# Stored key order inside each block of 128, one transfer back from DRAM instead of four, and an issue order that counts transfers instead of pieces

## The chip, the cores and the metric

The kernel runs on one core of one Trainium2 chip. The metric is the device time of one execution in microseconds (us); for the kernel before the change three runs gave 772.27, 773.07 and 774.95, median 773.07. Five engines work side by side, each with its own queue of instructions: PE (TensorE, matrix products), DVE (VectorE), ACT (ScalarE), POOL (GpSimd) and SP (SyncE). In this kernel SP does nothing but issue DMA transfers, all of them.

## The reference

One layer of a streaming encoder, for a prompt of 1024 positions and a sample of 32, in float32. `A` heads use band attention with a relative bias and a softmax, `B` heads use stick-breaking attention. Keys and values are also outputs.

```python
def band_attention(q, k, v, q_pos, k_pos, bias_table):
    s = jnp.einsum('bqhd,bkhd->bhqk', q, k).astype(jnp.float32) * ATTN_SCALE
    ...
    w = jax.nn.softmax(s, axis=-1).astype(v.dtype)
    return jnp.einsum('bhqk,bkhd->bqhd', w, v)

def stick_breaking(q, k, v, q_pos, k_pos):
    z = jnp.einsum('bqhd,bkhd->bhqk', q, k).astype(jnp.float32) * ATTN_SCALE
    causal = (k_pos[None, :] < q_pos[:, None])[None, None]
    log_beta = jax.nn.log_sigmoid(z)
    log_1m = jnp.where(causal, jax.nn.log_sigmoid(-z), 0.0)
    after = lax.cumsum(log_1m, axis=3, reverse=True) - log_1m
    w = jnp.where(causal, jnp.exp(log_beta + after), 0.0).astype(v.dtype)
    return jnp.einsum('bhqk,bkhd->bqhd', w, v)

def finish(h, oa, ga, ob, gb, w_out, g_post, p, w_ple, w_ple_gate):
    y = jnp.concatenate([oa * jax.nn.silu(ga), ob * jax.nn.silu(gb)], axis=-1) @ w_out
    h = h + rmsnorm(y, g_post)
    return h + jax.nn.sigmoid(h @ w_ple_gate) * (p @ w_ple)
```

In front of these stands an RMS norm and one projection to q, k, v and a gate for 8 `A` heads and 8 `B` heads of 64 columns.

## The kernel before

[...] Stage 0 norms and transposes x and starts the projection; stages 1 to 8 (`rec.stage`) each hold two attention heads of one kind (A, B, A, B ...) woven with the projection columns of the next pair, and in stage 8 with the gates; stages 9 to 13 are the output projection and the final gate. Names in the profile say the kind: `mm_kB` is a projection bank, `SB` a bank of scores, `ptwB` a bank of transposed weights, `PVB` the bank of weights times values.

**Weights and their transposition.** In a head the 1024 queries are eight blocks `i` of 128. `scores(i)` makes the scores of block `i` against up to 1024 keys (up to 640 for `A`) and from them the weights `w1` with queries on the partitions: for `A` a DVE reduction and an ACT exponential, for `B` two ACT sigmoids per bank, a DVE scan, and a POOL multiplication `be<-be`. Products with the values need the keys on the partitions, so `weights_t(i)` transposes, in one of two ways set by `ROUND`. Blocks `A` 0 to 4 and `B` 0 to 3 and 7 are transposed by PE into `ptw` banks. Blocks `A` 5, 6, 7 and `B` 4, 5, 6 (48 in all) go through DRAM: DVE turns squares of 32 by 32, one DMA stores the block (`swapA<-be`), and four DMAs bring it back (`be<-swapA`), one for each group of 32 keys, each to 32 partitions. ACT (`wTh<-be`) and DVE (`wTl<-be`) then split it. The values of each of the eight pairs make the same trip in `values_out` (`swapA<-vxA`, then four `stvA<-swapA`) and are then stored to the output by one DMA, `out_dram<-vt`.

**Order.** The program isn't run in the order in which it is written. A recorder collects all instructions with their dependences; `latest` works out a due time for each, and `simulate` then places them one at a time, per engine, by due time plus an offset from two tables (`AHEAD_OF`, and by stage `AHEAD_AT`), with estimated costs. `PASSES` is how often due times and placement are made anew. For SP, the planner before holds back a transfer while the pieces of those under way are over a limit:

```python
while away and (away[0][0] <= t or flying + o.pieces > AWAY):
    landed, pieces = heapq.heappop(away)
    flying -= pieces
    t = max(t, landed)
```

The queues are then fixed: an instruction that isn't ready holds up all that stand behind it on its engine. In the program as built each transfer also takes one of eight completion semaphores in turn, and SP waits before it issues a transfer until the one that had the semaphore before it is complete.

Of the kernel before, what the change touches and what calls it, by code (L numbers as in the profile page):

```python
# [10 lines left out]
AF = mybir.ActivationFunctionType  # L11
ALU = mybir.AluOpType

P = 128
# [14 lines left out]
    ('ACT', 'L'): -809, ('ACT', 'Qfs'): -495, ('ACT', 'S'): -671, ('ACT', 'be'): 45,  # L29
    ('ACT', 'gT'): 1145, ('ACT', 'junk'): -1222, ('ACT', 'o'): 225, ('ACT', 'oT'): -1406,  # L30
    ('ACT', 'om'): -82, ('ACT', 'ot'): -967, ('ACT', 'p'): -874, ('ACT', 'pleo'): -1053,
    ('ACT', 'sgg'): 65, ('ACT', 'stq'): -314, ('ACT', 'stv'): -824, ('ACT', 'v'): 55,
    ('ACT', 'wTh'): -117, ('ACT', 'whS'): 246, ('ACT', 'whs'): 933, ('ACT', 'x'): -696,
    ('ACT', 'xS'): -616, ('DVE', 'Kl'): -588, ('DVE', 'L'): 544, ('DVE', 'S'): -85,
    ('DVE', 'Vl'): -913, ('DVE', 'cc'): -493, ('DVE', 'diags'): -1253, ('DVE', 'g'): 212,
    ('DVE', 'h'): -1097, ('DVE', 'hnl'): 570, ('DVE', 'lg'): 343, ('DVE', 'om'): -53,
    ('DVE', 'ot'): -267, ('DVE', 'over'): 483, ('DVE', 'sgg'): -356, ('DVE', 'sq'): 277,
    ('DVE', 'stats'): -1190, ('DVE', 'uu'): 246, ('DVE', 'v'): -653, ('DVE', 'vx'): -722,
    ('DVE', 'w'): -1469, ('DVE', 'wTl'): 37, ('DVE', 'wl'): 652, ('DVE', 'wlS'): -1002,
# [3 lines left out]
    ('POOL', 'be'): 196, ('POOL', 'gT'): 309, ('POOL', 'o'): -123, ('POOL', 'ogg'): 890,  # L43
    ('POOL', 'om'): 197, ('POOL', 'rs'): -497, ('POOL', 's'): -1046, ('POOL', 'sgg'): 929,
# [4 lines left out]
}  # L49
AHEAD_AT = {  # L50
    (0, 'ACT', 'pleo'): 1195, (0, 'ACT', 'sq'): 1380, (0, 'ACT', 'stk'): -1095, (0, 'ACT', 'v'): 1160,
    (0, 'DVE', 'hnl'): -45, (0, 'DVE', 'rb'): 799, (0, 'DVE', 'sq'): 461, (0, 'DVE', 'x'): 572,
# [12 lines left out]
    (4, 'ACT', 'om'): -35, (4, 'ACT', 'wTh'): -365, (4, 'ACT', 'whs'): -1064, (4, 'DVE', 'S'): -89,  # L65
    (4, 'DVE', 'Ss'): 1254, (4, 'DVE', 'ot'): 307, (4, 'DVE', 'wTl'): -134, (4, 'PE', 'S'): 77,
    (4, 'PE', 'ptw'): 56, (4, 'PE', 'ptws'): -349, (4, 'POOL', 'ksS'): -959, (4, 'POOL', 'om'): 162,
    (4, 'POOL', 'w'): -151, (4, 'POOL', 'wl'): 1076, (4, 'SP', 'Kcs'): 477, (4, 'SP', 'be'): -112,
    (4, 'SP', 'o'): -577, (4, 'SP', 'wr'): -890, (5, 'ACT', 'be'): -546, (5, 'ACT', 'kd'): -484,
    (5, 'ACT', 'stk'): 1450, (5, 'ACT', 'wTh'): -482, (5, 'DVE', 'S'): -110, (5, 'DVE', 'om'): -127,  # L70
# [3 lines left out]
    (6, 'ACT', 'L'): 734, (6, 'ACT', 'be'): -459, (6, 'ACT', 'kd'): 409, (6, 'ACT', 'stv'): 1412,  # L74
# [4 lines left out]
    (7, 'ACT', 'om'): 64, (7, 'ACT', 'stk'): -573, (7, 'ACT', 'wTh'): -208, (7, 'DVE', 'Kcs'): 660,  # L79
# [6 lines left out]
    (8, 'POOL', 'ogg'): -1077, (8, 'POOL', 'om'): 190, (8, 'POOL', 'sgg'): -350, (8, 'POOL', 'w'): 324,  # L86
# [2185 lines left out]
```

## Time and profile before

| what | value |
|---|---|
| median of three runs | 773.07 us |
| the profiled execution: its time, its span | 773.43 us, 771.7 us |
| PE busy (matmuls) | 758.4 us, 98% |
| DVE, ACT, POOL busy | 611.6, 525.0, 447.2 us |
| DMA queue q1 | 172.70 MB, 77.1% of 16 engines' span |
| granted TensorE clock | 1.00 |

The page gives for each engine the time that it was busy. A matmul's end is modelled, so "busy" PE isn't yet PE at its pace: how fast matmuls follow one another is seen from their starts. SP isn't listed as busy on the page; its issues are seen in the timeline, as SPq. "Waits" rows say which engine and tile waited, for whom, for how long in all, how often, and how long at most. An issue row gives the size and the median time from issue to landing.

### The profile page before, as it was taken

How to read it: one execution, taken by the hardware profiler on the slowest of the kernel's cores; microseconds unless marked ns; L12 is line 12 of the kernel's file. 1: busy time of each engine (PE TensorE's matmuls, PEld its weight loads, DVE VectorE, ACT ScalarE, POOL GpSimd, SP SyncE). 2: the span in 40 equal slices, each digit the busy share in tenths (PEclk: the TensorE clock that was granted, in tenths of full speed). 3: DMA queues.
4: the chain of work that ended last, by engine and by line, in shares of the span. 5: the costliest groups of instructions: out<-in, count | busy, mean ns of one | idle time of the engine just before them, and what ended most of it. 6: DMA issues, size and time to landing. Idle time of an engine off the chain costs nothing.

```text
span 771.7 us, 14284 instructions
## 1 busy us (share of the span) xinstructions
PE 758.4 (98%) x4410; PEld 698.9 (91%) x4410; DVE 611.6 (79%) x1067; ACT 525.0 (68%) x1122; POOL 447.2 (58%) x503
## 2 busy tenths in 40 slices
PE   9999999999999999999999999999999999999997
PEld 7999999999989899999999999999998877888786
DVE  7837868878878898959898698698565688988965
ACT  6656776787766776866788586665347877884641
POOL 6624434751356682557874467679463448689533
PEclk9999999999999999999999999999999999999999
DMA  8658667476789858889799989897779866769664
GB/s 302 220 146 223 178 166 218 120 197 206 182 192 253 218 171 229 258 237 263 216 240 269 246 231 223 270 276 214 213 267 300 275 221 227 235 202 332 214 212 136
DMA packets 202333, 173.61 MB, mean 225 GB/s; under 512 B 66817, under 2 KB 164457, under 8 KB 202258
## 3 DMA queue, kind: packets, MB, share of 16 engines
q1 hardware_dynamic: 202258, 172.70, 77.1%
q8 instruction: 35, 0.57, 0.3%
q14 instruction: 40, 0.33, 0.1%
HBM read 105.46 MB, written 58.78 MB: 213 GB/s over the span
## 4 chain that ended last, share of the span: by engine, by line
PE 86%; DVE 4%; DMA 4%; SPq 3%; issue 1%; ACT 1%; DVEq 0%; POOL 0%; ACTq 0%; POOLq 0%
PE mm_gA L780 6%; PE mm_gB L780 6%; PE mm_kA L780 6%; PE mm_qA L780 5%; PE mm_kB L780 5%; PE mm_vA L780 5%; PE mm_qB L780 4%; PE PVB L780 4%; PE mm_vB L780 4%; PE SB L780 4%; PE PVA L780 3%; PE ple L780 3%; PE SA L780 3%; SPq L780 3%; PE g0P L780 3%; PE g2P L780 3%
## 5 line engine op out<-in xcount | busy, mean ns | idle before, releaser
L780 POOL TENSOR_TENSOR be<-be 128x128 f32<-128x128 f32 (+8 forms) x66 | 85.1, 1294 | 48.6 <-DVE be L780 23.0
L780 DVE TENSOR_TENSOR_SCAN be<-be,SB 128x384 f32<-128x384 f32 (+5 forms) x96 | 91.5, 963 | 8.2 <-ACT be L780 4.3
L780 ACT ACTIVATE be<-SB 128x384 f32<-128x384 f32 (+4 forms) x192 | 83.4, 497 | 18.2 <-DVE be L780 7.0
L780 DVE TENSOR_TENSOR wTl<-be,wTh 128x640 fp32r<-128x640 f32 (+2 forms) x48 | 51.9, 1086 | 11.2 <-ACT wTh L780 7.8
L780 ACT ACTIVATE be<-be,statA 128x640 f32<-128x640 f32 (+3 forms) x64 | 44.5, 696 | 11.6 <-DVE statA L780 11.5
L780 DVE STREAM_TRANSPOSE be<-be 128x640 f32<-128x640 f32 (+3 forms) x56 | 47.9, 866 | 3.4 <-POOL be L780 2.3
L780 ACT CAST wTh<-be 128x640 fp32r<-128x640 f32 (+2 forms) x48 | 37.6, 784 | 13.2 <-DMA be<-swapB 7.3
L780 PE MATMUL SB<-kdB,LB 128*128 128x384 f32 (+5 forms) x96 | 33.7, 354 | 0.4 <-issue 0.3
L780 PE MATMUL SB<-klB,LB 128*128 128x384 f32 (+5 forms) x96 | 33.3, 347 | 0.0
L780 DVE CUSTOM_DVE_ANT_0 be<-SA,biasA 128x320 f32<-128x320 f32 (+3 forms) x64 | 29.7, 481 | 4.4 <-PE SA L780 3.4
L780 POOL TENSOR_TENSOR gB<-gB,gB 128x256 f32<-128x256 f32 x32 | 26.9, 861 | 9.8 <-DMA gB<-in_w_ple_gate_dram 7.9
L780 ACT CAST wTh<-ptwB 128x512 fp32r<-128x512 f32 (+3 forms) x48 | 22.4, 484 | 13.0 <-PE PVB L780 8.0
L780 PE MATMUL SA<-kdA,LA 128*128 128x320 f32 (+2 forms) x96 | 30.3, 325 | 0.2 <-PE mm_kB L780 0.2
L780 PE MATMUL SA<-klA,LA 128*128 128x320 f32 (+2 forms) x96 | 30.1, 317 | 0.0
L780 POOL TENSOR_TENSOR oB<-oB,oB 128x256 f32<-128x256 f32 x32 | 25.6, 826 | 6.7 <-DMA oB<-in_w_out_dram 4.8
L780 PE MATMUL ptwB<-ident,be 128*128 128x128 f32 x144 | 26.5, 274 | 2.4 <-ACT be L780 1.0
L780 POOL TENSOR_TENSOR klB<-stkB,kdB 64x1024 fp32r<-64x1024 f32 x8 | 20.0, 2504 | 14.0 <-ACT kdB L780 12.1
L780 DVE TENSOR_TENSOR wTl<-ptwB,wTh 128x512 fp32r<-128x512 f32 (+3 forms) x48 | 25.0, 540 | 3.9 <-ACT wTh L780 3.7
L780 POOL TENSOR_TENSOR klA<-stkA,kdA 64x1024 fp32r<-64x1024 f32 (+2 forms) x9 | 19.3, 2150 | 14.4 <-ACT kdA L780 9.5
L780 DVE TENSOR_TENSOR wTl<-ptwA,wTh 128x128 fp32r<-128x128 f32 (+3 forms) x48 | 21.8, 478 | 5.3 <-ACT wTh L780 3.5
L780 DVE TENSOR_TENSOR LA<-stqA,LA 64x1024 fp32r<-64x1024 f32 (+2 forms) x9 | 15.6, 1730 | 11.9 <-ACT LA L780 11.8
L780 POOL TENSOR_TENSOR wl_vB<-wr_vB,wh_vB 128x512 fp32r<-128x512 f32 x8 | 10.5, 1309 | 24.5 <-DMA stvA<-swapA 13.3
(694 smaller groups left out, 2653.6 us busy)
## 6 DMA issues: line engine op xcount, KB each, us to landing
swapA<-be SPq DMA_DIRECT2D x24, 320.0 KB, 3.7
be<-swapA SPq DMA_DIRECT2D x96, 80.0 KB, 3.0
oB<-in_w_out_dram SPq DMA_DIRECT2D x16, 256.0 KB, 4.2
sum_dro<-oB SPq DMA_DIRECT2D x16, 256.0 KB, 3.2
gB<-in_w_ple_gate_dram SPq DMA_DIRECT2D x16, 256.0 KB, 3.9
sum_drg<-gB SPq DMA_DIRECT2D x16, 256.0 KB, 3.8
x<-in_x_prompt_dram SPq DMA_DIRECT2D x16, 256.0 KB, 3.9
h_dr<-h SPq DMA_DIRECT2D x8, 512.0 KB, 4.3
```

The costliest lines, as they stand in the source:

```text
L780: getattr(getattr(tc.nc, o.what[0]), o.what[1])(*args, **kw)
```

## The change

Three things change together.

1. **Key order.** Inside each block of 128 keys, key `32 c + q` now stands at place `4 q + c`. With it the four DMAs of a block become one to 128 partitions, for the 48 blocks of weights and for the eight pairs of values: 56 x 4 = 224 loads become 56. The store of values to the output, which must be in the old order, becomes four DMAs from every fourth partition in place of one: 8 become 32. In all, 970 DMAs become 826; the bytes and the pieces stay.
2. **Where PE transposes,** the weights must stand in the new order in `w1` before. For `A` 0 to 4 the exponential writes every fourth element (`mixed`), for `B` 0 to 3 and 7 the second sigmoid does, and the POOL multiplication reads one operand and writes its result so. These are 40 exponentials, 48 sigmoids and 40 multiplications.
3. **The planner** counts eight transfers (`LANES`) in place of pieces, has other DMA and issue constants, makes four passes in place of one, and both offset tables are new. So the order changes on every engine and in every stage. The instructions of PE, DVE, ACT and POOL are the same in number.

```diff
 AHEAD_OF = {
-    ('ACT', 'L'): -809, ('ACT', 'Qfs'): -495, ('ACT', 'S'): -671, ('ACT', 'be'): 45,
+    ('ACT', ''): 326, ('ACT', 'S'): -178, ('ACT', 'be'): 37, ('ACT', 'g'): 1215,
...
-ISSUE = 550
+ISSUE = 480
 TABLE = 1280
-DMA_START, DMA_DONE, DMA_RATE, DMA_MARGIN = 1950, 300, 320.0, 2000
-AWAY = 1900
+DMA_START, DMA_DONE, DMA_RATE, DMA_MARGIN = 1850, 1600, 320.0, 2100
+LANES = 8
...
-PASSES = 1
+PASSES = 4
...
-                while away and (away[0][0] <= t or flying + o.pieces > AWAY):
-                    landed, pieces = heapq.heappop(away)
-                    flying -= pieces
-                    t = max(t, landed)
+                if len(landed) >= LANES:
+                    t = max(t, landed[-LANES])
                 free[e] = t + o.busy
                 line = max(line, t + DMA_START) + o.late
-                heapq.heappush(away, (line + DMA_DONE, o.pieces))
-                flying += o.pieces
+                landed.append(line + DMA_DONE)
...
-            for c in range(4):
-                part = D[:, c * 256:(c + 1) * 256].rearrange("(g t) x -> t g x", t=32)
-                dma(st[32 * c:32 * c + 32, 0:SEQ].rearrange("t (g x) -> t g x", g=4), part)
+            dma(st[:, 0:SEQ].rearrange("p (g x) -> p g x", g=4), D.rearrange("(g t) (c x) -> (t c) g x", t=32, c=4))
...
-            later(o_p[0, 0, :, h2, :].rearrange("(b p) h d -> p b (h d)", p=P), out[:, b0:8, :])
+            rows = o_p[0, 0, :, h2, :].rearrange("(b c q) h d -> c q b (h d)", c=4, q=32)
+            for c in range(4):
+                later(rows[c], out[c::4, b0:8, :])
...
+    def split(x):
+        return x.rearrange("p (b c q) -> p b c q", c=4, q=32)
+
+    def mixed(x):
+        return x.rearrange("p (b q c) -> p b c q", c=4, q=32)
...
+                mix = mixed if i not in together else lambda x: x
                 for a, b, s in pieces:
-                    nc.scalar.activation(w1[:, a:b], s, AF.Sigmoid)
+                    nc.scalar.activation(mix(w1[:, a:b]), split(s) if i not in together else s, AF.Sigmoid)
...
-                nc.gpsimd.tensor_tensor(w1[:, 0:n], w1[:, 0:n], w0[:, 1:n + 1], ALU.mult)
+                if i in together:
+                    nc.gpsimd.tensor_tensor(w1[:, 0:n], w1[:, 0:n], w0[:, 1:n + 1], ALU.mult)
+                else:
+                    nc.gpsimd.tensor_tensor(mixed(w1[:, 0:n]), mixed(w1[:, 0:n]), split(w0[:, 1:n + 1]), ALU.mult)
...
-                nc.scalar.activation(w1[:, 0:n], w0[:, 0:n], AF.Exp, bias=m[:, last:last + 1], scale=-1.0, accum_out=r)
+                out, src = w1[:, 0:n], w0[:, 0:n]
+                if i not in together:
+                    out, src = mixed(out), split(src)
+                nc.scalar.activation(out, src, AF.Exp, bias=m[:, last:last + 1], scale=-1.0, accum_out=r)
...
-                for c in range(4):
-                    x = dr[:, c * m * 32:(c + 1) * m * 32].rearrange("(g k) x -> k g x", k=32)
-                    dma(w1[32 * c:32 * c + 32].rearrange("k (g x) -> k g x", g=4), x)
+                dma(w1.rearrange("p (g x) -> p g x", g=4), dr.rearrange("(g k) (c x) -> (k c) g x", k=32, c=4))
```

Two places show how rows move. The first is SP's queue in stage 5, at the second `A` head of pair 2, where the blocks 5, 6 and 7 of its weights come back (`swapA21_5` to `_7`; `x4` at a row's end is four DMAs). Before:

```order
L780 DMA swapA21_7_145<-be_178 128x640
L780 DMA o_dr2_65<-otA21_0_0_4359 64x256
L780 DMA klB21_4299<-klB21_4299 64x1024
L780 DMA be_178<-swapA21_5_143 32x4x160 x2
L780 DMA sum_dro_81<-oB212_4342 128x512
L780 DMA o_dr2_65<-otA20_1_0_4250 64x256
L780 DMA be_178<-swapA21_5_143 32x4x160 x2
L780 DMA oB123_4455<-in_w_out_dram 128x512
L780 DMA be_178<-swapA21_6_144 32x4x160 x4
L780 DMA oB223_4461<-in_w_out_dram 128x512
L780 DMA be_178<-swapA21_7_145 32x4x160 x4
```

The same place after:

```order
L767 DMA swapA21_7_145<-be_178 128x640
L767 DMA sum_dro_81<-oB212_4174 128x512
L767 DMA klB21_4284<-klB21_4284 64x1024
L767 DMA oB123_4335<-in_w_out_dram 128x512
L767 DMA oB223_4336<-in_w_out_dram 128x512
L767 DMA biassA1_4305<-r_dr_83 32x544
L767 DMA wr_vA3_0_4371<-in_w_in_dram 128x4x128
L767 DMA biassA1_4305<-r_dr_83 32x544
L767 DMA be_178<-swapA21_5_143 128x4x160
L767 DMA be_178<-swapA21_6_144 128x4x160
L767 DMA be_178<-swapA21_7_145 128x4x160
```

From the first load of block 5 to the last of block 7 there were 16 issues; now there are three, and most of the transfers that stood between them stand ahead of them.

The second place is ACT's queue a little later, where the first `B` head of pair 2 starts (`SB20_0` to `SB20_4` are its banks of scores) and the returned `A` weights are split (`wTh<-be`). Before:

```order
L780 ACTIVATE be_178<-SB20_0_0_4493 128x128
L780 ACTIVATE be_178<-SB20_1_0_4494 128x256
L780 CAST wTh_693<-be_178 128x4x5x32
L780 ACTIVATE be_178<-SB20_0_0_4493 128x128
L780 ACTIVATE be_178<-SB20_1_0_4494 128x256
L780 ACTIVATE be_178<-SB20_2_0_4531 128x384 x2
L780 CAST wTh_693<-be_178 128x4x5x32
L780 COPY stvB2_4129<-mm_vB2_1_4443 128x352
L780 CAST wTh_693<-ptwB20_0_0_4583 128x128
L780 ACTIVATE be_178<-SB20_3_0_4573 128x512 x2
L780 CAST wTh_693<-be_178 128x4x5x32
L780 CAST wTh_693<-ptwB20_1_0_4602 128x256
```

After:

```order
L767 ACTIVATE be_178<-SB20_0_0_4381 128x128
L767 ACTIVATE be_178<-SB20_1_0_4382 128x256
L767 COPY stvB2_4015<-mm_vB2_0_4280 128x352
L767 ACTIVATE be_178<-SB20_0_0_4381 128x4x32
L767 ACTIVATE be_178<-SB20_2_0_4420 128x384
L767 ACTIVATE be_178<-SB20_1_0_4382 128x2x4x32
L767 ACTIVATE be_178<-SB20_2_0_4420 128x3x4x32
L767 CAST wTh_667<-be_178 128x4x5x32
L767 ACTIVATE be_178<-SB20_3_0_4429 128x512
L767 CAST wTh_667<-be_178 128x4x5x32
L767 COPY stvB2_4015<-mm_vB2_1_4440 128x352
L767 COPY otA21_0_1_4513<-PVA21_0_4361 64x256
```

The first split of a returned block has moved behind four more of the sigmoids and a copy, and the sigmoids whose output is written with a step stand there in forms such as `128x3x4x32`.

More of the change, by code (lines that the diff above doesn't have):

```diff
@@ L44 @@
-    ('POOL', 'om'): 197, ('POOL', 'rs'): -497, ('POOL', 's'): -1046, ('POOL', 'sgg'): 929,
[4 rows of a table removed]
+    ('ACT', ''): 326, ('ACT', 'S'): -178, ('ACT', 'be'): 37, ('ACT', 'g'): 1215,
+    ('ACT', 'gT'): -586, ('ACT', 'kd'): 392, ('ACT', 'newh'): -442, ('ACT', 'oT'): -285,
+    ('ACT', 'om'): 12, ('ACT', 'ot'): -268, ('ACT', 'pleo'): 1103, ('ACT', 'sg'): 200,
+    ('ACT', 'sgg'): -312, ('ACT', 'stk'): 419, ('ACT', 'stv'): -751, ('ACT', 'whS'): 659,
+    ('ACT', 'whs'): -690, ('ACT', 'x'): -205, ('ACT', 'xS'): 903, ('DVE', 'Kcs'): 470,
@@ L86 @@
-    (8, 'POOL', 'ogg'): -1077, (8, 'POOL', 'om'): 190, (8, 'POOL', 'sgg'): -350, (8, 'POOL', 'w'): 324,
[3 rows of a table removed]
-    (10, 'POOL', 'r'): 153, (11, 'DVE', ''): -1125, (11, 'DVE', 'lg'): 155, (11, 'DVE', 'lo'): 1476,
-    (11, 'DVE', 'ug'): -230, (11, 'DVE', 'wl'): -51, (11, 'DVE', 'wlS'): 1328, (11, 'POOL', 'h'): -525,
-    (11, 'POOL', 'ms'): -252, (12, 'DVE', 'S'): 224, (12, 'DVE', 'cc'): 571, (12, 'POOL', 'gT'): -1069,
+    (0, 'ACT', 'hnh'): -601, (0, 'ACT', 'sq'): 800, (0, 'ACT', 'wh'): 1309, (0, 'DVE', 'hnl'): -712,
@@ new lines @@
+    (4, 'DVE', 'Vh'): -86, (4, 'DVE', 'newl'): 318, (4, 'DVE', 'om'): -38, (4, 'DVE', 'v'): -458,
[3 rows of a table added]
+    (6, 'ACT', 'stk'): -96, (6, 'ACT', 'wTh'): 141, (6, 'DVE', 'om'): -126, (6, 'DVE', 'vx'): 665,
+    (6, 'PE', 'PV'): 41, (6, 'PE', 'S'): -608, (6, 'PE', 'ptw'): 65, (6, 'POOL', 'be'): 481,
+    (6, 'POOL', 'g'): 425, (6, 'SP', 'g'): 1322, (6, 'SP', 'sum'): -598, (7, 'ACT', 'be'): -55,
+    (7, 'ACT', 'newh'): 1337, (7, 'ACT', 'om'): 262, (7, 'ACT', 'ot'): 393, (7, 'ACT', 'wTh'): 736,
+    (7, 'DVE', 'diags'): 667, (7, 'DVE', 'newl'): 442, (7, 'DVE', 'om'): -81, (7, 'DVE', 'vx'): 1151,
@@ new lines @@
+    (7, 'PE', 'mm'): 21, (7, 'PE', 'ptr'): 667, (7, 'PE', 'ptxs'): 66, (7, 'POOL', 'g'): 224,
+    (7, 'SP', 'o'): 13, (7, 'SP', 'sum'): 478, (8, 'ACT', 'be'): -104, (8, 'ACT', 'om'): -416,
+    (8, 'ACT', 'sgg'): -751, (8, 'ACT', 'w'): 1359, (8, 'DVE', 'Kcs'): -401, (8, 'DVE', 'Kl'): 793,
+    (8, 'DVE', 'S'): 420, (8, 'DVE', 'Vl'): 955, (8, 'PE', 'PV'): 402, (8, 'PE', 'S'): -509,
+    (8, 'PE', 'ptw'): -404, (8, 'PE', 'ptxs'): -1224, (8, 'POOL', 'be'): 508, (8, 'POOL', 'sgg'): 48,
+    (8, 'SP', 'Kcs'): 399, (8, 'SP', 'og'): 238, (8, 'SP', 'swap'): 850, (8, 'SP', 'wr'): 305,
@@ L93 @@
+    (9, 'ACT', ''): 572, (9, 'ACT', 'wh'): 174, (9, 'ACT', 'xS'): -115, (9, 'PE', 'ple'): 451,
[3 rows of a table added]
+    (12, 'ACT', 'gT'): 980, (12, 'ACT', 'whS'): 844, (12, 'ACT', 'xS'): 1318, (12, 'DVE', 'cc'): 441,
+    (12, 'DVE', 'gj'): 313, (12, 'DVE', 'uu'): 634, (12, 'PE', 'g'): 1304, (12, 'POOL', 'gT'): -88,
+    (12, 'POOL', 'ug'): 336, (12, 'SP', 'hh'): 361, (12, 'SP', 'to uu'): -753, (13, 'PE', 'g'): 503,
 }
@@ L705, in leave @@
                 come(new.place, b.gone)
-        out, port, line, table, away, flying, last = [], 0.0, 0.0, AF.Exp, [], 0, 0.0
+        out, port, line, table, landed, last = [], 0.0, 0.0, AF.Exp, [], 0.0
         while len(out) < len(self.ops):
```

45 lines of the change are left out of this document (18 added, 27 removed), and 41 rows, old and new, of tables (AHEAD_AT, AHEAD_OF).

## The prediction, on record before the change was run

> **What bounds the kernel now.** I read the page's busy times first, then the waits of PE, then the timelines of SP, ACT and PE at the places that the waits name. The page:
>
> ```profile
> span 771.7 us, 14284 instructions
> PE 758.4 (98%) x4410; PEld 698.9 (91%) x4410; DVE 611.6 (79%) x1067; ACT 525.0 (68%) x1122; POOL 447.2 (58%) x503
> ```
>
> PE is busy for 758.4 of 771.7 us, and the change leaves its 4410 matmuls as they are. So the time can fall only by what PE loses in waits, and can rise by as much as new waits add. This is what PE waited for in the whole execution, all rows (total us, times, longest):
>
> ```profile
> PE ptwA L780 <- DVE statA L780: 1.3, 1, 1.3
> PE idle L780 <- DVE newh L780: 1.3, 1, 1.3
> PE SsB L780 <- DVE QlsB L780: 1.1, 1, 1.1
> PE ptwB L780 <- ACT be L780: 1.0, 2, 0.7
> PE ptwB L780 <- ACT stvB L780: 0.9, 1, 0.9
> PE PVB L780 <- DMA be<-in_cache_a_k_dram: 0.5, 1, 0.5
> PE mm_vB L780 <- DVE diagsA L780: 0.3, 1, 0.3
> PE ptwB L780 <- DVE over L780: 0.3, 1, 0.3
> PE SB L780 <- issue: 0.3, 1, 0.3
> PE SsA L780 <- ACT QhsA L780: 0.2, 1, 0.2
> PE ptwB L780 <- POOL be L780: 0.2, 1, 0.2
> PE o2P L780 <- DVE h L780: 0.2, 1, 0.2
> PE SA L780 <- PE mm_kB L780: 0.2, 1, 0.2
> ```
>
> They come to 7.8 us. The `idle` row is the start of the program, so 6.5 us are within reach. That is a small prize, 0.8% of the time, and the first thing the reader should take from the profile.
>
> **Where these waits come from.** The rows of `ptwB` for ACT and POOL fall in one place, between 342 and 350 us, the place shown in the orders above. SP's queue there, with the loads of returned `A` weights:
>
> ```profile
> 333.31 1.45 SPq L780 DMA_DIRECT2D be<-swapA  x2
> ...
> 335.87 1.99 SPq L780 DMA_DIRECT2D be<-swapA  x2
> 337.90 0.43 SPq L780 DMA_DIRECT2D oB<-in_w_out_dram  x1
> 338.37 1.85 SPq L780 DMA_DIRECT2D be<-swapA  x4
> ...
> 340.74 1.86 SPq L780 DMA_DIRECT2D be<-swapA  x4
> ```
>
> SP issues one transfer after another with hardly a pause, about 0.47 us each (1.85 us for four, and a gap to the next row). The loads of three blocks take it from 333.31 to 342.60, 9.3 us. ACT stands behind them:
>
> ```profile
> 343.49 0.73 ACT L780 CAST wTh<-be 128x640 fp32r<-128x640 f32 x1 [1.95 <-DMA be<-swapA]
> ```
>
> This split of the second block waits at the head of ACT's queue, with copies and sigmoids behind it, and PE waits for those:
>
> ```profile
> 342.07 0.33 PE L780 MATMUL ptwB<-ident,be 128*128 128x128 f32 x1 [0.22 <-POOL be L780]
> ...
> 344.72 0.30 PE L780 MATMUL ptwB<-ident,be 128*128 128x128 f32 x1 [0.87 <-ACT stvB L780]
> ...
> 347.91 0.97 PE L780 MATMUL mm_kA<-hnh,wh_kA 128*128 128x352 f32 x5
> 349.56 0.30 PE L780 MATMUL ptwB<-ident,be 128*128 128x128 f32 x1 [0.68 <-ACT be L780]
> ```
>
> The largest row, `ptwA` for DVE at 444.30, goes back by the chain to a late load issued in another crowd of SP's. First the chain's row, then SP's:
>
> ```profile
> 437.67 5.12 DMA vnsA<-vs_drA
> ```
>
> ```profile
> 430.39 2.01 SPq L780 DMA_DIRECT2D be<-swapA  x4
> ...
> 437.20 0.96 SPq L780 DMA_DIRECT2D vnsA<-vs_drA  x2
> ```
>
> So SP's queue, which no busy row shows, stands behind 0.2 + 0.9 + 0.7 + 1.3 us. I add `PVB`, which waited for a transfer (0.5), and `SsA`, for ACT (0.2), as probably of the same kind: 3.8 us.
>
> **The transfers.** 168 loads go and 24 stores come: 144 issues fewer, at 0.47 us some 68 us of SP's queue. How long the merged load takes isn't in the trace. The rows nearest to it (KB each, us from issue to landing):
>
> ```profile
> swapA<-be SPq DMA_DIRECT2D x24, 320.0 KB, 3.7
> be<-swapA SPq DMA_DIRECT2D x96, 80.0 KB, 3.0
> ...
> be<-in_x_prompt_dram SPq DMA_DIRECT2D x4, 512.0 KB, 6.5
> ```
>
> Before, the last of four landed 3 x 0.47 + 3.0 = 4.4 us after the first issue. One transfer of 320 KB took 3.7 in the other direction, and I take that value, since the size is the same; the ends are 3.0 and 6.5. A block comes back 0.7 us earlier, and at the place above the third one does 16 - 3 = 13 issues, 6 us, earlier. The 24 added stores are 11 us of SP, included in the 68; they are at low priority, but one that stands in the queue holds it for 0.47 us, and what stands behind is then the next load. In what it does for PE I count the 3.8 us. A PE wait costs more than its row says: the five `mm_kA` from 347.91 start 0.16 us apart (four gaps to a sixth start at 348.72), and PE began again at 349.56, 0.84 late where the row says 0.68. These are six waits, and 0.15 more for each makes 0.9. **Gain: 4.7 us**, between 0 (others take their place) and 6.5 + 13 x 0.15 = 8.4.
>
> **The steps in memory.** 40 multiplications on POOL now read one operand and write with a step of four elements. Five widths of eight each, 44.4 us in all; the widest and the narrowest:
>
> ```profile
> L780 POOL TENSOR_TENSOR be<-be 128x1024 f32<-128x1024 f32 x8 | 17.7, 2217 | 9.9 <-DVE be L780 7.0 <-DVE SB L780 2.0 <-ACT be L780 0.7
> L780 POOL TENSOR_TENSOR be<-be 128x128 f32<-128x128 f32 x8 | 4.3, 533 | 6.4 <-ACT be L780 4.8 <-DVE be L780 1.5
> ```
>
> No POOL or ACT instruction of the trace steps over elements. The nearest that does is a DVE transposition, which reads with a step of eight and writes with one of four (`fetch_T`), beside one whose squares lie in rows:
>
> ```profile
> L780 DVE STREAM_TRANSPOSE ug<-ht 128x1024 f32<-128x1024 f32 x4 | 9.1, 2275 | 0.0
> L780 DVE STREAM_TRANSPOSE be<-be 128x896 f32<-128x896 f32 x8 | 8.8, 1098 | 2.3 <-POOL be L780 2.3
> ```
>
> 1098 x 1024 / 896 = 1255, so the step cost a factor of 1.8. The ends are 1.0 (a step is free, and a gain has no reason) and 1.8. For POOL I take 1.4, between them, since one of its two inputs has no step; for ACT 1.0, since only its output has one, with 1.8 as the end. POOL then works 44.4 x 0.4 = 18 us more. What hides this is the time between the end of a multiplication and the transposition that reads it. The widest blocks have the most to lose, and here are the tightest that I found and an ordinary one:
>
> ```profile
> 496.85 2.10 POOL L780 TENSOR_TENSOR be<-be 128x1024 f32<-128x1024 f32 x1 [0.78 <-DVE be L780]
> ```
>
> ```profile
> 499.52 1.03 PE L780 MATMUL ptwB<-ident,be 128*128 128x128 f32 x8
> ```
>
> ```profile
> 289.93 2.19 POOL L780 TENSOR_TENSOR be<-be 128x1024 f32<-128x1024 f32 x1 [0.74 <-ACT be L780]
> ```
>
> ```profile
> 294.88 0.49 PE L780 MATMUL ptwB<-ident,be 128*128 128x128 f32 x3
> ```
>
> The cover is 499.52 - 498.95 = 0.57 us in the one and 294.88 - 292.12 = 2.76 in the other. 2.2 x 0.4 = 0.9 us more passes the first by 0.3 and stays inside the second. **Cost: 1.0 us**, for three such tight blocks, between 0 and, at 1.8 and with the cover of 0.57 in all eight widest blocks, 8 x (1.8 - 0.57) = 9.8.
>
> [...]
>
> **The new order.** It moves every engine's rows at no cost of its own, and whether its waits are fewer can't be read from rows without times; that is why the lower end of the gain is 0. The stages after 595 us hold one PE wait of 0.2 and can gain nothing.
>
> **The sum.** 773.43 - 4.7 + 1.0 = 769.7 for the profiled execution, which is 0.36 over the median; so about **769.4**, 0.5% faster.
>
> **Rivals.**
> *The steps bite: slower.* With the factor 1.8 on POOL the widest block is 1.8 us later, and if ACT has it too, its two sigmoids of 512 add 0.5 each (row below): 2.8 us in the path from score to transposition. The mean of the covers above is 1.7, so 1.1 us of PE is lost in each of eight heads, 9 us, and the DVE that shares the work of these blocks is pushed too, which the narrower ones (32 of them, 0.4 to 1.0 us more) would show: if a quarter of these stalls PE by 0.5, 4 more. 773.1 - 4.7 + 13 = 781. It decides from an added delay above 1.7 us. For it speaks the DVE row; against it that PE waited for POOL once, 0.2 us in all. [...]
>
> ```profile
> L780 ACT ACTIVATE be<-SB 128x512 f32<-128x512 f32 x48 | 26.9, 602 | 7.2 <-DVE SB L780 3.1 <-DVE be L780 1.8 <-PE SB L780 1.2
> ```
>
> *Waits change places: no change.* The queues are fixed by estimates in both kernels, the loads were late for other reasons (SP's stores wait for DVE and POOL at its head), or the merged load lands after 6.5 us. As many waits as before: 773 give or take 2.
> *Nearly all waits go.* If planned and real transfers agree better, the 8.4 us go and little is added: 765. Against it: `SsB` and `mm_vB` wait for DVE, which the change doesn't relieve.
>
> **How the numbers follow.** About 0.3%, 2.3 us, is what a measurement can tell from no change. Chances: the forecast 0.35, nearly all waits gone 0.17, no change 0.16, slower 0.32 (of this a third beyond 783). Faster by over 0.3% is 0.52. The range runs from 762 (8.4 us and some short gaps less) to 783, and leaves out 0.03 below and 0.11 above; the forecast's own range is 766 to 771.
>
> **What the profile after would show.** For the first term: SP's rows `be<-swapA` single and landing in about 3.7 us, ACT's waits for them shorter than 1.95, and PE's waits for ACT at the start of the `B` heads gone. For the second: the `be<-be` rows of 1024 at about 3.1 us. Wrong would be: a merged load over 4.4 us; PE rows `ptwB` waiting for POOL `be` by several us; or long waits for DVE or ACT at places where before there were none, which would be the new order's own.

## The result: 1.1% slower, and the profile after

The changed kernel takes 781.86 us (median of four runs, 781.70 to 782.17), the kernel before 772.93 beside it: a ratio of 1.0111 with a 95% interval of 1.0093 to 1.0130. The profiled execution's span is 779.9 us, before it was 771.7.

The page of the kernel after, span and busy times:

```profile
span 779.9 us, 13988 instructions
PE 761.2 (98%) x4410; PEld 697.1 (89%) x4410; DVE 624.5 (80%) x1067; ACT 548.2 (70%) x1122; POOL 466.2 (60%) x503
```

ACT is busy for 23 us more, POOL for 19, DVE for 13, with the same number of instructions. What PE waited for after (total us, times, longest), the longest rows:

```profile
PE SB L767 <- DVE be L767: 2.0, 4, 1.0
PE ptwA L767 <- DVE statA L767: 1.8, 1, 1.8
PE ptwB L767 <- POOL be L767: 1.7, 5, 0.6
PE SA L767 <- DVE LA L767: 1.5, 1, 1.5
PE idle L767 <- DVE newh L767: 1.3, 1, 1.3
PE ptp L767 <- DMA pp<-in_p_prompt_dram: 1.1, 1, 1.1
PE SsA L767 <- ACT QhsA L767: 0.8, 1, 0.8
```

All rows come to 12.9 us, where they were 7.8. Of the rows that the prediction went after, those of `ptwB` for ACT's `be` and `stvB` are gone; the largest, `ptwA` for `statA`, is still there and has grown from 1.3 to 1.8. Others have come, and most name DVE or POOL. The rows hold only a part of the loss. Counted by the starts of matmuls, as the time by which the next start comes over 40 ns later than the median for this tile and shape, PE lost 30.2 us before and 38.3 after: 8.1 us, nearly all of the 8.2 by which the spans differ.

The groups that the change touches, after:

```profile
L767 POOL TENSOR_TENSOR be<-be 128x1024 f32<-128x1024 f32 x8 | 24.3, 3033 | 11.0 <-ACT be L767 4.7 <-ACT otB L767 3.2 <-issue 1.2
L767 ACT ACTIVATE be<-SB 128x512 f32<-128x512 f32 x48 | 39.2, 860 | 10.0 <-DVE SB L767 3.6 <-POOL be L767 3.1 <-POOL wl_kB L767 2.0
L767 ACT ACTIVATE be<-be,statA 128x512 f32<-128x512 f32 x8 | 9.8, 1230 | 0.0
L767 DVE TENSOR_TENSOR wTl<-be,wTh 128x640 fp32r<-128x640 f32 x32 | 41.2, 1293 | 5.3 <-ACT wTh L767 5.3
```

Two of the same groups before, which the prediction did not show:

```profile
L780 ACT ACTIVATE be<-be,statA 128x512 f32<-128x512 f32 x8 | 5.8, 723 | 1.1 <-DVE statA L780 1.1
L780 DVE TENSOR_TENSOR wTl<-be,wTh 128x640 fp32r<-128x640 f32 x32 | 32.1, 1008 | 9.2 <-ACT wTh L780 6.4 <-DMA be<-swapB 2.5 <-DMA gB<-in_w_ple_gate_dram 0.3
```

A multiplication of 1024 with the step takes 3033 ns where it took 2217, a factor of 1.37. An exponential of 512 takes 1230 where it took 723, 1.70. Of the 48 sigmoids of 512 half have the step; their mean went from 602 to 860, so the stepped ones take about 860 x 2 - 602 = 1118, 1.86 times as long. The last row is a surprise: DVE's subtraction `wTl<-be` (the low part of the weights: `be` less its high part `wTh`) has no step and was not changed, yet it takes 1293 ns in place of 1008.

The transfers, after (KB each, median us from issue to landing), and ACT's waits for them:

```profile
swapA<-be SPq DMA_DIRECT2D x24, 320.0 KB, 4.0
be<-swapA SPq DMA_DIRECT2D x24, 320.0 KB, 5.1
```

```profile
ACT wTh L767 <- DMA be<-swapA: 3.5, 6, 1.2
ACT wTh L767 <- DMA be<-swapB: 2.3, 3, 0.9
```

The merged load lands in 5.1 us. From the first issue to the last landing a block took a median of 4.85 us before and 4.83 after, over the blocks whose last landing is in the trace (29 and 30 of 48): a block is back no sooner after its first issue. Yet ACT's waits for returned blocks fell from 12.9 us (5.6 for `A`, 7.3 for `B`) to 5.8.

### The profile page after: what moved, and what is told of

It is laid out like the page before. It is cut to its first block, busy times and chain, and to the rows that moved or that the text cites. A ratio compares the mean times of both kernels' runs of the same rounds, so it can differ in the third digit from the quotient of the medians.

```text
span 779.9 us, 13988 instructions
## 1 busy us (share of the span) xinstructions
PE 761.2 (98%) x4410; PEld 697.1 (89%) x4410; DVE 624.5 (80%) x1067; ACT 548.2 (70%) x1122; POOL 466.2 (60%) x503
## 5 line engine op out<-in xcount | busy, mean ns | idle before, releaser
L767 POOL TENSOR_TENSOR be<-be 128x384 f32<-128x384 f32 (+8 forms) x66 | 102.6, 1563 | 38.0 <-DVE be L767 21.4
L767 ACT ACTIVATE be<-SB 128x512 f32<-128x512 f32 (+5 forms) x192 | 101.5, 600 | 27.6 <-DVE be L767 8.9
L767 DVE TENSOR_TENSOR_SCAN be<-be,SB 128x384 f32<-128x384 f32 (+4 forms) x96 | 91.6, 962 | 17.2 <-ACT be L767 7.4
L767 ACT ACTIVATE be<-be,statA 128x640 f32<-128x640 f32 (+4 forms) x64 | 57.9, 933 | 10.9 <-DVE statA L767 8.3
L767 DVE TENSOR_TENSOR wTl<-be,wTh 128x640 fp32r<-128x640 f32 (+2 forms) x48 | 60.3, 1258 | 5.6 <-ACT wTh L767 5.5
L767 DVE CUSTOM_DVE_ANT_0 be<-SA,biasA 128x320 f32<-128x320 f32 (+2 forms) x64 | 29.4, 480 | 5.8 <-issue 4.1
L767 POOL TENSOR_TENSOR h<-h,x 128x512 f32<-128x512 f32 (+1 forms) x18 | 24.2, 1352 | 1.4 <-DVE h L767 1.4
L767 PE MATMUL PVB<-wTl,v2B 128*128 128x512 f32 (+1 forms) x96 | 23.6, 347 | 0.0
L767 PEld LDWEIGHTS SB<-kdB,LB 128*128 128x128 f32 x96 | 18.0, 188 | 6.1 <-DVE be L767 3.5
```

What stands on the lines that cost most here:

```text
L767: getattr(getattr(tc.nc, o.what[0]), o.what[1])(*args, **kw)
```

## The experiments

Three theories: the **steps** cost more than forecast (theory S in the texts below); the new **order** has a cost of its own (theory O); the **gain** of single transfers never came (theory N, against theory G, by which it is real, and about as forecast, in an order that stays). Each ratio is to the kernel before, run on the same chip, with its 95% interval.

| kernel | order | transfers back | step | ratio |
|---|---|---|---|---|
| after | after | 1 | 4 elements, ACT and POOL | 1.0111 [1.0093, 1.0130] |
| e1 | planner of before | 1 | 4, ACT and POOL | 1.0398 [1.0371, 1.0425] |
| e2 | planner of after | 4 | none | 1.0137 [1.0112, 1.0163] |
| e3 | after | 1 | none | 1.0017 [0.9997, 1.0037] |
| e4 | before | 4 | 4, ACT and POOL | 1.0047 [1.0024, 1.0070] |
| e5 | after | 1 | 4, POOL only | 1.0042 [1.0018, 1.0066] |
| e6 | after | 1 | 4, ACT only | 1.0099 [1.0070, 1.0129] |
| e7 | before | 1 | none | 0.9921 [0.9895, 0.9946] |
| e8 | before | 1 | 4, ACT and POOL | 1.0052 [1.0035, 1.0068] |
| e9 | before | 2, apart | 2, ACT and POOL | 1.0000 [0.9989, 1.0011] |
| e10 | before | 2, apart | none | 0.9978 [0.9966, 0.9990] |
| e11 | before | 1 | 4, moved to PE for `A` 0 to 3 | 1.0057 [1.0038, 1.0077] |
| e12 | before | 2, together | 2, ACT and POOL | 0.9990 [0.9976, 1.0005] |
| e13 | before | 2, together, stores spread | 2, ACT and POOL | 0.9977 [0.9964, 0.9991] |
| e14 | before | 1, stores spread | 4, ACT and POOL | 1.0036 [1.0021, 1.0050] |

Where the order is that of before and transfers are fewer, the planner placed the old instructions and the transfers were exchanged when the program was put out, so every row of PE, DVE, ACT and POOL stands where it stood.

### The planner and the tables: e1 and e2

e1 is the kernel after with the planner's rules, constants and both tables of before:

```diff
-LANES = 8
+AWAY = 1900
...
-PASSES = 4
+PASSES = 1
```

> The changed kernel with the planner of before: its tables, constants, one pass, pieces counted. Key order, single transfers and steps in memory stay. If the steps in memory cost the time (theory S), this one is slow too, 778 to 786 us. If the new order costs it (theory O), this one keeps what the fewer transfers bring, 768 to 773 us.

e2 is the kernel before with the rules, constants and tables of after:

```diff
-AWAY = 1900
+LANES = 8
...
-PASSES = 1
+PASSES = 4
```

> The kernel before with the new planner and tables alone; four loads for each block, no steps. Theory S: no slower than before, 768 to 774 us. Theory O: slower, 778 to 786 us.

804.05 and 784.09 us. Both are slower than both kernels; e1 lies outside both ranges that were written down, e2 inside that of theory O. e1 does the same work as e8 below, which keeps the order of before and takes 1.0052, so most of its 4% is the order that the old tables give for a program with fewer transfers. The tables of each kernel seem to fit only the program that they stand in. So neither run says what the planner's rule is worth, and to take the parts apart the order must be held still.

### The steps, in the order of after: e3, e5, e6

e3 has all of the change but the steps (so weights meet values in another key order where PE transposes; the instructions and transfers are the same):

```diff
     def split(x):
-        return x.rearrange("p (b c q) -> p b c q", c=4, q=32)
+        return x
     def mixed(x):
-        return x.rearrange("p (b q c) -> p b c q", c=4, q=32)
+        return x
```

> The changed kernel in exactly its own order, but ACT and POOL write the weights without a step, so that the key order is left out there and the attention output is of wrongly paired keys. ACT's exponentials and sigmoids and POOL's multiplications go back to their durations of before. Theory S: 768 to 773 us, 9 to 13 us below the changed kernel. Theory O: 779 to 782 us, unchanged.

773.93 us, some 7 us below the kernel after, where theory S had 9 to 13: the steps are worth 1.0111 / 1.0017, 0.94% or 7.3 us. e5 and e6 put them back in one engine. e5, whose exponentials lose the step as well:

```diff
-                    nc.scalar.activation(mix(w1[:, a:b]), split(s) if i not in together else s, AF.Sigmoid)
+                    nc.scalar.activation(w1[:, a:b], s, AF.Sigmoid)
```

> The changed kernel in its own order with the step in POOL's multiplications alone; ACT writes without a step, so the output pairs wrong keys. ACT's step added 23 us to ACT's busy time and POOL's 19 to POOL's. If ACT's step makes most of the 8 us (theory S-ACT): 774 to 776 us. If POOL's does (theory S-POOL): 779 to 782 us.

e6:

```diff
-                    nc.gpsimd.tensor_tensor(mixed(w1[:, 0:n]), mixed(w1[:, 0:n]), split(w0[:, 1:n + 1]), ALU.mult)
+                    nc.gpsimd.tensor_tensor(w1[:, 0:n], w1[:, 0:n], w0[:, 1:n + 1], ALU.mult)
```

> The changed kernel in its own order with the step in ACT's exponentials and sigmoids alone, POOL without one (wrong pairs again). S-ACT: 778 to 781 us. S-POOL: 774 to 776 us.

Both leave the key order out where one engine writes without the step. POOL's step alone adds 0.25 points to e3, with intervals that overlap; ACT's alone adds 0.82, nearly all. DVE tells the two apart. First e5, the step on POOL alone:

```profile
L767 DVE TENSOR_TENSOR wTl<-be,wTh 128x640 fp32r<-128x640 f32 x32 | 37.1, 1164 | 4.4 <-ACT wTh L767 4.2
L767 POOL TENSOR_TENSOR be<-be 128x1024 f32<-128x1024 f32 x8 | 24.8, 3103 | 5.7 <-DVE be L767 3.9 <-ACT be L767 1.1 <-POOL be L767 0.3
```

and e6, the step on ACT alone:

```profile
L767 DVE TENSOR_TENSOR wTl<-be,wTh 128x640 fp32r<-128x640 f32 x32 | 34.9, 1097 | 5.6 <-ACT wTh L767 5.3
L767 POOL TENSOR_TENSOR be<-be 128x1024 f32<-128x1024 f32 x8 | 16.8, 2100 | 10.9 <-ACT be L767 4.6 <-ACT otB L767 3.1 <-issue 1.2
```

In e3 the first row has 1063. DVE's busy time is 612.4 us in e3, 611.7 in e6 and 620.8 in e5: it is POOL's step that makes DVE slower here. Places where a row of DVE grows beside a multiplication are shown below, at e8. With both steps the row is at 1293, more than the two add up to one by one.

### The order of before held: e4, e7, e8

e4 is the kernel before with the steps alone; four loads bring blocks back in the old order, so blocks that PE transposes meet values in another key order.

```diff
-                nc.gpsimd.tensor_tensor(w1[:, 0:n], w1[:, 0:n], w0[:, 1:n + 1], ALU.mult)
+                if i in together:
+                    nc.gpsimd.tensor_tensor(w1[:, 0:n], w1[:, 0:n], w0[:, 1:n + 1], ALU.mult)
+                else:
+                    nc.gpsimd.tensor_tensor(mixed(w1[:, 0:n]), mixed(w1[:, 0:n]), split(w0[:, 1:n + 1]), ALU.mult)
```

> The kernel before in its own order and with its own transfers, with the steps in ACT's and POOL's weights alone (again wrongly paired keys in the output). Theory S: 780 to 786 us. Theory O: 772 to 775 us.

777.67 us, between the two ranges: here the steps cost 0.47%, 3.6 us (1.9 to 5.4).

e7 is the kernel before with single transfers alone: at the place of the first of four loads stands the whole one, the other three are left out, and a store of values is four. The key order is left out where PE transposes, as in e3.

```diff
                     dma(w1[32 * c:32 * c + 32].rearrange("k (g x) -> k g x", g=4), x)
+                    full = w1.rearrange("p (g x) -> p g x", g=4), dr.rearrange("(g k) (c x) -> (k c) g x", k=32, c=4)
+                    rec.ops[-1].instead = [] if c else [full]
```

> The kernel before in its own order, row for row, but of the four loads of a block only the first is issued and it fetches the whole block; the other three are left out, and each store of values is four. No steps in memory, so wrong pairs. If SP's queue stood behind the 3.8 us of PE waits that the prediction charged to it (theory G): 767 to 770 us, and the waits of PE for ACT near 345 us are gone. If the transfers bring nothing (theory N): 772 to 775 us.

767.55 us, 0.79% or 6.1 us faster (4.2 to 8.1): the gain is real. The two kernels run PE's matmuls in the same order, so their starts can be laid side by side. e7's lead grows from 1.3 us at 322 us of the kernel before to 3.7 at 362, and from 3.7 at 403 to 6.7 at 464; over the rest it moves by little, 1.3 us up to the first of these. These are the two places that the prediction named. At the first, the load of the third block is issued at 334.62 us where it was at 340.74, and lands at 342.22 where its last part landed at 345.95. PE's waits in e7, the longest first:

```profile
PE idle L785 <- DVE newh L785: 1.3, 1, 1.3
PE SsB L785 <- DVE QlsB L785: 1.1, 1, 1.1
PE ptwB L785 <- ACT be L785: 0.4, 1, 0.4
```

All rows come to 3.3 us. And e3 is e7's work in the order of after: 1.0017 / 0.9921 = 1.0097. **The new order costs about 7.5 us by itself** (some 5 to 10 by the two intervals). The longest waits in e3:

```profile
PE SB L767 <- DVE be L767: 2.0, 2, 1.8
PE SsA L767 <- ACT QhsA L767: 1.9, 1, 1.9
PE SB L767 <- ACT stkA L767: 1.7, 1, 1.7
```

They stand in several places and name two engines, and the execution profiled took 776.5 us, 2.6 over the median of e3; no single cause was found, and which entry of the tables makes them was not tried.

e8 is e7 with the steps, so the whole key order in the order of before, and complete:

```diff
+                mix = mixed if i not in together else lambda x: x
...
-                    nc.scalar.activation(w1[:, a:b], s, AF.Sigmoid)
+                    nc.scalar.activation(mix(w1[:, a:b]), split(s) if i not in together else s, AF.Sigmoid)
```

> The run before this with the steps in ACT's and POOL's weights: the whole key order, with the right output, in the row order of before, with the old tables and planner. From the 4.7 us that the steps cost in this order: theory G 771 to 775 us, theory N 776 to 780 us.

777.6 us, in the range of theory N, although e7 has shown the gain: the steps take 1.0052 / 0.9921, 1.3% or 10 us, the whole gain and more. In the same order, but with four loads, they took 3.6 (e4). So the parts don't add up: with the steps in, the single transfers bring nothing that can be told from zero (e8 over e4, 1.0052 / 1.0047). Laid beside e7, e8 loses 5.1 us of its 10.0 at one place, where a `B` head ends and an `A` head starts. In the timelines there, POOL, DVE and PE of e8:

```profile
401.53 3.52 POOL L785 TENSOR_TENSOR be<-be 128x1024 f32<-128x1024 f32 x1
```

```profile
401.34 0.92 DVE L785 TENSOR_TENSOR wTl<-be,wTh 128x640 fp32r<-128x640 f32 x1 [1.05 <-ACT wTh L785]
402.29 3.83 DVE L785 TENSOR_TENSOR LA<-stqA,LA 64x1024 fp32r<-64x1024 f32 x1
```

```profile
408.06 0.42 PE L785 MATMUL SA<-kdA,LA 128*128 128x320 f32 x1 [3.23 <-DVE statA L785]
```

and the same `LA` and the multiplication in e7:

```profile
396.12 1.65 DVE L785 TENSOR_TENSOR LA<-stqA,LA 64x1024 fp32r<-64x1024 f32 x1
```

```profile
396.65 2.98 POOL L785 TENSOR_TENSOR be<-be 128x1024 f32<-128x1024 f32 x1
```

In e8 DVE's `LA` starts while the stepped multiplication runs and ends at 406.12, 1.07 us after POOL's end at 405.05. An `LA` of this form that met no POOL instruction took 1.22 us (before, at 156.76), so by an estimate from these rows DVE did next to none of it until POOL was through, and behind `LA` stood the reduction (`statA`) for which PE waits. In e7 `LA` started first, 0.53 us ahead of the multiplication, and it was POOL that took longer, 2.98 us where its mean is 2.22. In e8 `LA` came 0.76 behind, after a split (`wTl`) that had waited 1.05 us for ACT. So at this place ACT's lateness and POOL's length work together; the steps of the two engines were not run apart in this order.

The kernel after has the same signature. Its PE wait of 1.5 us for `LA` stands behind these two, which end at 400.92 (POOL) and 402.00 (DVE), 1.08 later:

```profile
398.00 2.92 POOL L767 TENSOR_TENSOR be<-be 128x1024 f32<-128x1024 f32 x1 [0.32 <-ACT be L767]
```

```profile
398.75 3.25 DVE L767 TENSOR_TENSOR LA<-stqA,LA 64x1024 fp32r<-64x1024 f32 x1 [2.01 <-ACT LA L767]
```

And a 640 wide `wTl<-be` takes 0.78 to 0.83 us when POOL is idle, while this one, behind a multiplication that ends at 165.85, takes 3.44 and ends 0.67 after it:

```profile
163.08 3.44 DVE L767 TENSOR_TENSOR wTl<-be,wTh 128x640 fp32r<-128x640 f32 x1
```

```profile
162.62 3.23 POOL L767 TENSOR_TENSOR be<-be 128x1024 f32<-128x1024 f32 x1 [0.65 <-ACT be L767]
```

So in three places a DVE subtraction that ran beside a multiplication of POOL took 3.25 to 3.83 us and ended 1.07, 1.08 and 0.67 us after POOL's end; what joins the two engines there, the rows do not show. The split of 512 columns that has one of its inputs in PSUM (`wTl<-ptwB`) kept its time: 676 ns before, 679 after.

The wait of 3.23 us is not all that PE loses there. Stretches of e8 (busy us and instructions of PE, its weight loads, DVE, ACT and POOL, then the granted clock, DMA share and GB/s):

```profile
404.00:408.00 4.00, 0.82 (x6) 0.54 (x4) 3.94 (x5) 1.23 (x1) 3.67 (x4) 1.00 0.92 248
408.00:411.00 3.00, 2.94 (x14) 2.94 (x15) 2.55 (x10) 2.96 (x9) 3.00 (x4) 0.57 0.91 244
411.00:414.00 3.00, 3.00 (x19) 2.98 (x19) 1.94 (x7) 3.00 (x4) 2.22 (x2) 0.86 0.89 186
414.00:417.00 3.00, 3.00 (x20) 2.77 (x20) 2.85 (x8) 1.16 (x5) 0.00 (x0) 1.00 1.10 299
```

After the wait the granted clock is 0.57 for three microseconds and 0.86 for three more, some 3 x 0.43 + 3 x 0.14 = 1.7 us. Shorter waits were followed by this too, but not all of them: in e2, behind a wait of 1.35 us, eight `mm_vA` started 0.27 us apart where six of the same width started 0.16 apart six microseconds later, and in e3 one of 1.92 was followed by a clock of 0.53, while in the kernel after one of 1.81 and in e14 one of 2.38 were followed by 1.00. So the length of a wait alone does not tell whether the clock falls behind it; what does, these runs do not show.

### A smaller step, and PE in ACT's place: e9, e10, e11

With two transfers a block can be mixed in halves of 64 keys, and the step is two elements. e9:

```diff
     def split(x):
-        return x.rearrange("p (b c q) -> p b c q", c=4, q=32)
+        return x.rearrange("p (b c q) -> p b c q", c=2, q=32)
     def mixed(x):
-        return x.rearrange("p (b q c) -> p b c q", c=4, q=32)
+        return x.rearrange("p (b q c) -> p b c q", c=2, q=32)
...
+                    half = w1[32 * c:32 * c + 64].rearrange("p (g x) -> p g x", g=4), drt[c // 2].rearrange("(g k) (c x) -> (k c) g x", k=32, c=2)
+                    rec.ops[-1].instead = [] if c % 2 else [half]
```

> The order of before row for row, but two transfers per block instead of four: keys are mixed in halves of 64, place 64 h + 2 q + c for key 64 h + 32 c + q, so ACT and POOL write with a step of two elements (8 bytes) where the whole change has four (16 bytes). The block is stored to DRAM in two halves so that each load is one plain pattern. Output complete. Theory 'the price goes by the size of the step': a step of two is free or nearly so, exponentials of 512 take under 0.85 us and multiplications of 1024 under 2.4, and the kernel keeps most of what the single transfers gave: ratio to before 0.992 to 0.996. Rival 'any step costs the same': exponentials of 512 about 1.2 us, multiplications of 1024 about 3.0, ratio 1.003 to 1.007.

e10 is e9 without `split` and `mixed`:

```diff
-                nc.scalar.activation(out, src, AF.Exp, bias=m[:, last:last + 1], scale=-1.0, accum_out=r)
+                nc.scalar.activation(w1[:, 0:n], w0[:, 0:n], AF.Exp, bias=m[:, last:last + 1], scale=-1.0, accum_out=r)
```

> As the kernel with two transfers and the step of two, but ACT and POOL write without a step (so blocks that PE transposes meet keys in another order than the values; this part of the computation is wrong, its time is what counts). It gives the worth of two transfers alone. If the gain goes with the issues that are gone, two give two thirds of what one transfer gave (0.9921): 0.994 to 0.996. If only the landing of the last quarter counts, about the same 0.992 to 0.993. Theory 'a step of two is free': within 0.2 points of the kernel with the step of two; rival 'any step costs': 1 to 1.3 points below it.

In e9:

```profile
L785 ACT ACTIVATE be<-be,statA 128x512 f32<-128x512 f32 x8 | 6.1, 760 | 1.6 <-DVE statA L785 1.6
L785 POOL TENSOR_TENSOR be<-be 128x1024 f32<-128x1024 f32 x8 | 21.0, 2623 | 11.1 <-DVE be L785 4.9 <-DVE SB L785 3.1 <-DMA oB<-in_w_out_dram 2.3
```

A step of two costs ACT 5% (760 against 724 in e10) and POOL 18% (2623 against 2224, more than the 2.4 us that were written down), and the kernel 0.22 points, where a step of four cost 1.3. But the forecast of 0.992 to 0.996 for e9 was too good, and e10's was as well: two transfers without a step gained 0.22%, and neither 0.4 to 0.6 nor 0.7 to 0.8. Ahead of its splits of returned blocks ACT waited 14.7 us in e9, 3.0 in e7, and a wait of 2.8 us of PE came of it.

e11 is e8 with the step of 32 of the 40 exponentials moved to the score matmuls (the relative bias stays in the old order for these blocks, so the key order is left out of it):

```diff
-                nc.tensor.matmul(s, lhs, kd[:, ks], start=True, stop=False)
+                turn = (lambda x: x.rearrange("p (b c q) -> p b q c", c=4, q=32)) if ab == "A" and i < 4 else (lambda x: x)
+                nc.tensor.matmul(s, lhs, turn(kd[:, ks]), start=True, stop=False)
```

> The order of before row for row, single transfers and the whole key order as in the kernel that gave 1.0052, but for the A blocks 0 to 3 the step is moved from ACT's exponential to PE: the score matmuls read the keys with a step of four elements, so the exponential writes without one (the relative bias is left in the old order for these blocks; that part of the computation is wrong). If PE reads a step at no cost, 32 of 40 exponentials are back at 0.72 us for 512 and the ratio falls by a third to a half of the steps' 1.3 points, to 0.998 to 1.001. If PE pays for a step as ACT does, its 128 matmuls of these blocks take 1.5 times as long, some 10 us more on the bound engine: 1.015 or above.

The exponentials are back at 723 ns and ACT is busy for 541.8 us, 4.9 less than in e8, but a matmul of 512 takes 444 ns where it took 404, and the ratio stays, 1.0057 against 1.0052: neither outcome that was written down. By their starts the stepped matmuls (64, not 128) cost PE some 1.4 us, an estimate from the medians of each width. That is a part only of what was to be won. The wait of `SA` for `statA` stands in e11 almost as in e8, 3.1 us for 3.2. So in this order either the step of these exponentials costs little, or other losses took its place; the run does not tell which.

### What stands ahead of the loads: e12, e13, e14

e12 issues both loads of a block at the place of the first:

```diff
-                    rec.ops[-1].instead = [] if c % 2 else [half]
+                    rec.ops[-1].instead = [] if c else halves
```

> As the kernel with two transfers and a step of two elements (ratio 1.0000), output complete, but both loads of a block are issued one right behind the other at the place of the first of four, where before the second stood at the third's place, behind other transfers. In the trace of the kernel without this PE lost 2.8 us once for ACT's QhsA, which stood behind a split that waited 2.48 us for a late second load, and ACT waited 14.7 us for returned blocks, where with one transfer it waited 3.0. Theory 'what counts is when the last part is back': that wait goes and ACT's waits come down towards 3 to 6 us; ratio 0.994 to 0.997, and with it a kernel faster than both. Rival 'only the number of issues counts': no change from 1.000.

0.9990: the waits ahead of ACT's splits fell from 14.7 to 8.9 us, not to 3 to 6, and the ratio by 0.1 points, inside the intervals. SP's queue in e12, at the place where ACT's wait comes from:

```profile
418.82 3.29 SPq L780 DMA_DIRECT2D out_dram<-vtA  x4
422.16 1.26 SPq L780 DMA_DIRECT2D be<-swapA  x2
```

The four stores of values stand in a row for 3.29 us right ahead of the loads; the one store in their place before took 0.39 us of SP. e13 issues the second, third and fourth of them 5, 10 and 15 transfers later:

```diff
-                    for dst, src in o.instead:
-                        tc.nc.sync.dma_start(dst.get(), src.get())
+                    for k, (dst, src) in enumerate(o.instead):
+                        if len(o.instead) == 4 and k:
+                            hold.append((issued + 5 * k, dst.get(), src.get()))
+                        else:
+                            tc.nc.sync.dma_start(dst.get(), src.get())
```

> As the kernel with both loads of a block issued at once and a step of two elements (ratio 0.9990), output complete, but of the four stores of values that replace one, the second, third and fourth are issued 5, 10 and 15 transfers later than the first. In the trace of that kernel the four stood in a row for 3.29 us on SP's queue right ahead of the loads that ACT and then PE waited for (1.4 us for QhsA). Theory 'the added stores hold the loads': ACT's waits for returned blocks fall from 8.9 us to under 5, PE's wait for QhsA goes, and the ratio falls to 0.994 to 0.997, a kernel faster than both. Rival 'the two loads are held by their own number': no change, 0.998 to 1.000.

e14 does the same to e8:

```diff
+                if o.eng == "SP":
+                    issued += 1
+                    while hold and hold[0][0] <= issued:
+                        tc.nc.sync.dma_start(*hold.pop(0)[1:])
```

> As the whole key order in the order of before (single transfers, step of four, ratio 1.0052), output complete, with the four stores of values spread in the same way. Theory 'steps make its loss': ACT hardly waits for returned blocks there (1.2 us), so nothing changes: 1.003 to 1.007. Rival 'the added stores make a part of it': the small losses at the heads of the second and third pair go, 0.998 to 1.002.

e13 is at 0.9977 (7.2 us of waits ahead of ACT's splits, PE's for `QhsA` gone), e14 at 1.0036. Each is 0.13 to 0.16 points below its partner, with intervals that overlap: e13 lies between the two ranges written down, and e14 in that of the theory by which spreading changes nothing there. A part of the difference can be the clock: at the place shown for e8, the wait of `SA` is 2.38 us in e14, and the granted clock behind it stays at 1.00 where it fell to 0.57. That the added stores hold up loads is likely, not shown. e13 computes all that the reference asks and has the lowest ratio of the complete kernels here: 0.23% under the kernel before, and 1.3% under the one after (0.9977 / 1.0111).

## Why the prediction was wrong

The forecast was 769.4 us with 762 to 783 as the range, the result 781.86: inside the range, on the other side of no change. In parts, by the runs: single transfers -6.1 us (e7), the order +7.5 (e3 over e7), the steps +7.3 (after over e3), together +8.7, and 8.9 between the medians. That these agree proves nothing, since each part starts from where the last one ended. Taken in another sequence the parts are others: the steps alone +3.6 (e4), the single transfers then +0.4 (e8 over e4), the order then +4.5 (after over e8). So the sum was wrong in one more way: it added a gain and a cost as if neither changed the other.

- **The gain, 4.7 us, was right where nothing else changes.** e7 has 6.1 (4.2 to 8.1), at the places named and as described: ACT's splits at the head of its queue wait less for returned blocks (2.5 us in all, where it was 12.9). The landing was mis-sized (5.1 where 3.7 was taken, over the 4.4 that was to refute it), and the 0.7 us by which a block was to come back sooner did not come. What is left is SP's queue, and there the third block was issued 6.1 us earlier (1.3 of it the lead that e7 had by then), close to the prediction's 6. With the steps in, the gain was not seen.
- **The step that failed first is "for ACT 1.0, since only its output has one".** Measured are 1.5 to 1.7 for the exponentials from 256 to 512 and about 1.86 for the sigmoids of 512, 23 us of ACT that the sum held at nothing. By e6 this is most of the steps' price in the order of after; the whole term "Cost: 1.0 us" came out at 7.3 there, and at 3.6 and 10 in the order of before. The nearest row of the trace, DVE's transposition with 1.8, was there and was set aside by an argument about inputs that no row bore out.
- **POOL's 1.4 was right** (1.34 to 1.41 for widths from 256 to 1024). Its way to PE was only half seen: the sum counted the cover between a multiplication and the transposition that reads it, for three blocks, and left out what becomes of DVE meanwhile (in e8 an `LA` of 3.83 us where e7 has 1.65).
- **"At no cost of its own" for the new order failed too.** The sum gave it nothing, and the lower end of the gain, 0, was to hold it. Without the steps it is 7.5 us, more than the whole gain. The prediction named such waits, "long waits for DVE or ACT at places where before there were none", as a sign, but gave them no price. Where in the order they come from stays open.
- **The slower rival** gave 781 and hit the time, with the steps on both engines as its mechanism. It priced them at 13 us and kept the gain; measured are 4 to 10, and the order made up the rest, which it did not speak of. So that it met the time is in part luck. Its chance of 0.32 was low: the row that spoke for it was the only one with a step.

## What to carry to other kernels

Price a step in an access pattern on each engine that gets it, from the nearest row that has one, and let no engine off for a reason without a row: a step of 16 bytes made ACT's and POOL's instructions of 256 columns and more 1.3 to 1.9 times as long here, one of 8 bytes 1.04 to 1.2. Beside POOL's longer instructions DVE's subtractions of two SBUF tiles grew longer too (with both steps in: `wTl<-be` of 640 columns 1293 ns in the kernel after, 1063 in e3, and `LA` of 1024 2221 ns in e8, 1918 in e7), so the price of a step on POOL is to be looked for in DVE's rows and not in POOL's waits alone. And where a change comes with a new order, hold the order and change the rest before believing either: here the transfers alone were worth 0.8%, about as forecast, and either the steps or the new order was enough to take it back. Run the parts together as well as one by one: a gain measured alone was gone once another part was in.

## What the runs showed of the hardware

- One transfer of 320 KB to 128 partitions landed in 5.1 us, each of four of 80 KB to 32 partitions in 3.0; from first issue to last landing the block took 4.83 and 4.85.
- A matmul with a moving operand of 512 columns read with a step of 16 bytes took 444 ns (e11), without one 404 (e8).
- A wait of PE can cost again what it lasted: in e9 2.8 us of waiting came to 5.6 us beside e7, with the granted clock at 0.50 and 0.56 in the six microseconds behind it, which is 3 x 0.50 + 3 x 0.44 = 2.8 us more (busy us and matmuls of PE, granted clock, DMA share, GB/s). It need not: behind 2.38 us in e14 the clock was 1.00.

```profile
434.00:437.00 3.00, 3.00 (x13) 0.50 0.83 220
437.00:440.00 3.00, 3.00 (x15) 0.56 0.51 154
440.00:443.00 3.00, 3.00 (x21) 1.00 0.71 153
```
